# Output projection of a hybrid decoder block: half of its k tiles by seven block products

## The chip, the cores and the metric

The kernel runs on one core of one Trainium2 chip. The core has five engines that work side by side, each in the order of its own queue: TensorE (PE, matmuls), VectorE (DVE), ScalarE (ACT), GpSimd (POOL) and SyncE (SP, which here issues DMAs). The metric is the time of one execution in microseconds; lower is better.

## The reference, cut to what matters

One decoder layer for 512 tokens of width 1024. Two token mixers (a gated MLP and a sparse attention) are each projected to width 1024, merged by sigmoid gates, and sent through one output projection; a gated residual follows, then a second norm and the FFN. Everything is float32.

```
merged = sigmoid(g_a) * (y_a @ w_proj_a) + sigmoid(g_b) * (y_b @ w_proj_b)
x = x + gate1 * (merged @ w_out)                       # 512 x 1024 @ 1024 x 1024
h2 = rms_norm(x, norm2_g) * (1.0 + scale2) + shift2
f_g, f_u = split(h2 @ w_ffn_in)
x = x + gate2 * ((silu(f_g) * f_u) @ w_ffn_out)
```

## The kernel before

**Split products.** To keep float32 precision each operand is split into a high and a low part (`split`, L302: ScalarE copies the high part, VectorE subtracts it from the source for the low part), and `mm3` (L51) does three matmuls for one product: high x high, high x low, low x high. So every weight chunk needs two elementwise passes before TensorE can use it.

**The weight stream.** Weight chunks of 512 KB, and between them pieces of `w_ada` for the modulation vectors, stand in one list, `stream`, in the order of their use. `issue` (L72) puts a load on SP's queue into one of three `raw` buffers. `prep` (L95) makes the high and low part: into one of three rotating `hi`/`lo` pairs, or into a home of its own (`where`). `get(i)` (L142) hands out chunk i and, before that, makes sure (`ensure`, L117) that all entries up to two weight chunks ahead are prepared. So the order in which `prep`'s instructions lie on ScalarE's and VectorE's queues follows from where `get` is called. A buffer is known by its tag (`S2_2`, `E5`); a new tile on a tag waits until the last instruction that reads the old one, wherever that stands in the program.

**The order around the change.** The instructions of each engine run in the order in which the program lists them.

- Attention with `gb_part` (L1018) as filler ends with four sigmoids of the branch gates (L1064).
- *Projection B* (L1089): four groups of 256 output channels. In each, `opt_b` (L668) goes through two weight chunks (k tiles 0 to 3, then 4 to 7) with 24 matmuls each, the weights stationary and `yb` moving, all 512 tokens in one matmul. `yb` lies in the tiles with tags S2_0 to S2_7: high parts of k tiles 4 to 7 in S2_2 and S2_3, low parts in S2_6 and S2_7. After the second chunk `pb_evac` (L1075) multiplies by the gate, adds the other branch's part (`part`), and splits the merged tile into `mT`. `sec_tasks` (L362) does transposes of modulation pieces and a VectorE reduction into `Gc`; it has two such tasks in this stage. Low halves of the first chunk of each group are made on GpSimd (`pool=True`, L258), the others on VectorE.
- Then the pool `mid`, which holds the tiles of the first half of the program, is closed and the pool `ffn` opened on its memory (L1092).
- *Output projection* (L1239): merged tokens stationary, weights moving, 512 columns a matmul. Two halves of the tokens, in each of them two column halves `h` and four pairs of k tiles: 192 matmuls in 16 steps of 12. `resid` (L1101) multiplies by the gate, adds to the residual stream `xt` and squares for the norm. In the second half `row_rstd`, `norm2_x` and `norm2_T` (L1108 to L1130) normalise and transpose the first half's tokens; `norm2_T(0)` stands after the third of eight steps. `ensure(WF0[...])` and `s_prep` (L1194) prepare the first FFN weights there.
- *FFN input* (L1463) begins with the first half's tokens, and `norm2_T(1)` stands after 72 of its matmuls.

The FFN input and the first part of the FFN output run already by seven products instead of eight (`sprod` L1491, `zprod` L1592): with operands cut into 2 x 2 blocks, sums and differences of blocks are made beforehand, and results that several output blocks share are copied by ScalarE from one PSUM bank into another (`z_copy`) or kept in SBUF and added by VectorE (`z_add`).

## Time and profile before

| | |
|---|---|
| runs of the kernel before | 837.93, 837.97, 838.38 us (median 837.97) |
| the profiled execution | 838.1 us, of which the span of instructions is 836.2 |
| mean granted TensorE clock | 0.998 |
| HBM read and written | 105.90 MB, 2.10 MB |
| projection B | 396.1 to 441.2 us of the span |
| output projection | 441.2 to 487.4 us of the span |

A row of the timeline gives the start in us, the duration, the engine, the line of the kernel, the operation, output <- inputs, the shape and the count of instructions that were merged into the row; what stands in brackets is how long the engine had been idle before it and what ended that. A merged row's duration runs from the first start to the last end. A matmul's duration includes its way through the array, so two in a row overlap: their distance is read from the starts.

### The profile page before, as it was taken

The numbers are of one execution on the slowest core, as the hardware profiler recorded it, in microseconds if no ns is written. First come the engines' busy times: TensorE is split into PE (matmuls) and PEld (weight loads), VectorE is DVE, ScalarE is ACT, GpSimd is POOL, SyncE is SP. The second block draws the span as 40 slices with busy tenths as digits, with TensorE's granted clock in tenths as the row PEclk, the third lists the DMA queues.
The fourth block names the chain that finished last, engine by engine and source line by source line (L and its number), as shares of the span: only waits on it lengthen the run. The fifth ranks groups of instructions, "written<-read, shape, count | busy, mean of one in ns | idle before, by whom it ended". The sixth has DMA issues, their size and how long they took to land.

```text
span 836.2 us, 12860 instructions
## 1 busy us (share of the span) xinstructions
PE 824.3 (99%) x4992; PEld 733.8 (88%) x4992; DVE 666.7 (80%) x1147; ACT 401.8 (48%) x700; POOL 118.3 (14%) x105
## 2 busy tenths in 40 slices
PE   7999999999999999999999999999999999999996
PEld 7888989988888888988888899999999999888885
DVE  7968799788899638887786679889998888985635
ACT  6664435332232227665433556555555555663322
POOL 2060022353344411002210000000000000000001
PEclk9999999999999999999999999999999999999999
DMA  9962362423346551036544312445543335143212
GB/s 299 311 193 67 101 200 79 127 79 97 102 151 200 171 183 51 26 102 229 172 153 155 97 51 78 127 158 164 169 139 103 101 101 151 52 150 101 76 50 101
DMA packets 95676, 109.09 MB, mean 130 GB/s; under 512 B 5616, under 2 KB 76272, under 8 KB 95616
## 3 DMA queue, kind: packets, MB, share of 16 engines
q1 hardware_dynamic: 92512, 101.37, 38.8%
q0 software_dynamic: 2384, 6.10, 2.0%
q8 instruction: 39, 0.64, 0.3%
q10 hardware_dynamic: 720, 0.82, 0.3%
q14 instruction: 21, 0.17, 0.1%
HBM read 105.90 MB, written 2.10 MB: 129 GB/s over the span
## 4 chain that ended last, share of the span: by engine, by line
PE 95%; DMA 2%; SPq 1%; issue 0%; ACT 0%; DVE 0%; POOLq 0%; POOL 0%; ACTq 0%
PE pb L53 9%; PE pb L55 9%; PE pb L54 9%; PE R L53 8%; PE R L54 8%; PE R L55 8%; PE pfo L55 4%; PE pfo L53 4%; PE pfo L54 4%; PE pav L54 2%; PE pav L53 2%; PE pav L55 2%; PE pgb L53 2%; PE po L54 2%; PE pgb L54 2%; PE pgb L55 2%
## 5 line engine op out<-in xcount | busy, mean ns | idle before, releaser
L110 ACT ACTIVATE hi<-raw 128x1024 fp32r<-128x1024 f32 (+2 forms) x83 | 85.6, 1035 | 106.5 <-PE pfo L55 35.3
L114 POOL TENSOR_TENSOR lo<-raw,hi 128x1024 fp32r<-128x1024 f32 x33 | 83.3, 2528 | 212.7 <-ACT hi L110 199.1
L114 DVE TENSOR_TENSOR lo<-raw,hi 128x1024 fp32r<-128x1024 f32 (+2 forms) x43 | 53.3, 1244 | 51.0 <-ACT hi L110 50.9
L53 PE MATMUL pb<-h,hi 128*128 128x512 f32 x192 | 76.4, 398 | 0.0
L55 PE MATMUL pb<-h,lo 128*128 128x512 f32 x192 | 75.8, 395 | 0.0
L54 PE MATMUL pb<-hl,hi 128*128 128x512 f32 x192 | 75.8, 395 | 0.0
L55 PE MATMUL pfo<-hi,gs 128*128 128x512 f32 (+1 forms) x126 | 46.4, 369 | 0.0
L54 PE MATMUL pfo<-lo,gs 128*128 128x512 f32 (+1 forms) x126 | 46.4, 368 | 0.0
L53 PE MATMUL pfo<-hi,gs 128*128 128x512 f32 (+1 forms) x126 | 46.4, 368 | 0.0
L53 PE MATMUL R<-tb,sx 128*128 128x256 f32 x160 | 45.2, 282 | 0.0
L54 PE MATMUL R<-tb,sx 128*128 128x256 f32 x160 | 45.1, 282 | 0.0
L55 PE MATMUL R<-tb,sx 128*128 128x256 f32 x160 | 45.0, 281 | 0.0
L55 PE MATMUL R<-tb,lo 128*128 128x256 f32 x160 | 44.8, 280 | 0.0
L53 PE MATMUL R<-tb,hi 128*128 128x256 f32 x160 | 44.8, 280 | 0.0
L54 PE MATMUL R<-tb,hi 128*128 128x256 f32 x160 | 44.6, 279 | 0.0
L55 PEld LDWEIGHTS pb<-h,lo 128*128 128x128 f32 x192 | 36.0, 187 | 8.8
L54 PEld LDWEIGHTS pb<-hl,hi 128*128 128x128 f32 x192 | 36.0, 188 | 8.3
L53 PEld LDWEIGHTS pb<-h,hi 128*128 128x128 f32 x192 | 36.0, 188 | 8.3
L175 DVE SCALAR_TENSOR_TENSOR acc<-mraw,cols,acc 128x512 f32<-128x512 f32 x38 | 32.4, 853 | 8.3 <-DMA mraw<-in_w_ada_dram 7.5
L54 PE MATMUL pav<-lo,h 128*128 128x256 f32 x128 | 35.8, 279 | 0.0
L53 PE MATMUL pav<-hi,h 128*128 128x256 f32 x128 | 35.7, 279 | 0.0
L55 PE MATMUL pav<-hi,hl 128*128 128x256 f32 x128 | 35.7, 279 | 0.0
(377 smaller groups left out, 2647.9 us busy)
## 6 DMA issues: line engine op xcount, KB each, us to landing
raw<-in_w_ffn_in_dram SPq DMA_DIRECT2D x44, 512.0 KB, 4.3
raw<-in_w_in_dram SPq DMA_DIRECT2D x40, 512.0 KB, 3.7
mraw<-in_w_ada_dram SPq DMA_DIRECT2D x22, 512.0 KB, 3.8
raw<-in_w_ffn_out_dram SPq DMA_DIRECT2D x17, 512.0 KB, 3.6
s<-in_w_ada_dram SPq DMA_DIRECT2D x30, 256.0 KB, 5.6
raw<-in_w_ada_dram SPq DMA_DIRECT2D x10, 512.0 KB, 4.6
raw<-in_w_proj_a_dram SPq DMA_DIRECT2D x8, 512.0 KB, 4.7
raw<-in_w_proj_b_dram SPq DMA_DIRECT2D x8, 512.0 KB, 3.3
```

The costliest lines, as they stand in the source:

```text
L53: T.matmul(o, wh, rh, start=start, stop=False, **kw)
L54: T.matmul(o, wh, rlo, start=False, stop=False, **kw)
L55: T.matmul(o, wlo, rh, start=False, stop=stop, **kw)
L110: A.activation(hi[:, :m], e["raw"][:, :m], AF.Copy)
L114: e["lo"].tensor_sub(lo[:, :m], e["raw"][:, :m], f(hi[:, :m]))
L175: V.scalar_tensor_tensor(o, w, cs[:, j:j + 1], o, op0=OP.mult, op1=OP.add)
```

## The change

*Weights.* The stream keeps only the output weights of k tiles 4 to 7, four chunks; two of them get homes on the tags S2_2, S2_3 and S2_6, S2_7. The weights of k tiles 0 to 3 are four blocks B11, B12, B21, B22 (two k tiles by 512 columns), loaded at the start of projection B by four DMAs of their own (`o_issue`) into tiles of `mid`. The low halves of all projection-B chunks are made on VectorE.

*Preparation.* Eight steps (`O_STEPS`), one behind each chunk of projection B, make the differences of the weight blocks and of the merged token blocks, and split those that are needed first: B11, T1, A11, S1, T2, S2, A12, B21. `pb_evac` writes the merged result into `part` itself, and splits only k tiles 4 to 7.

*Products.* Seven products of 12 matmuls each (`oprod`), with copies between PSUM banks (`seed`), two kept results (`keep`, `add_kept`), and the remaining splits between them. The pool `mid` is closed after the seventh.

*The other k tiles* come on top, first half of the tokens, then second, with four steps of 12 matmuls in each; `norm2_T(0)` stands after the third step of the second half.

```diff
--- before.py
+++ after.py
@@ -101,6 +101,8 @@
         if e["where"] is None:
             hi = base.tile([128, 1024], F32R, name="hi", tag="hi", bufs=3)
             lo = base.tile([128, 1024], F32R, name="lo", tag="lo", bufs=3)
+        elif isinstance(e["where"], tuple):
+            hi, lo = (base.tile([128, 1024], F32R, name="wx", tag=t, bufs=1) for t in e["where"])
         else:
             t = ffn[0].tile([128, 2, 1024], F32R, name="wx", tag=e["where"], bufs=1)
             hi, lo = t[:, 0], t[:, 1]
@@ -255,10 +257,10 @@
         W_PA.append(group(w_pa, 256 * g, mods=mm_ if g < 3 else None, pool=2))
     W_GB = [group(w_in, 5192 + 256 * g, pool=2 * (g == 1), mods=mm_ if g > 1 else None, mraw=False) for g in range(4)]
     stream[W_GB[1][0]]["lo"] = V
-    W_PB = [group(w_pb, 256 * g, pool=True, mods=mm_ if g < 3 else None, mraw=False) for g in range(4)]
-    W_O = []
-    for n_, (h, k0) in enumerate(((0, 0), (1, 0), (0, 2), (1, 2), (0, 4), (0, 6), (1, 4), (1, 6))):
-        W_O.append((h, add_w(w_o, [k0, k0 + 1], 512 * h, 512, V, (None, None, None, "E2", "E0", "E1", "E3", "E4")[n_])))
+    W_PB = [group(w_pb, 256 * g, mods=mm_ if g < 3 else None, mraw=False) for g in range(4)]
+    W_O = [add_w(w_o, [k0, k0 + 1], 512 * h, 512, V, where) for h, k0, where in
+           ((0, 4, ("S2_2", "S2_3")), (0, 6, ("S2_6", "S2_7")), (1, 4, None), (1, 6, None))]
     mg = mod_sec(5)
     wh = ["E5", "E6", "E0", "E1"]
     W_F = [group(w_ffn_in, c, where=wh) for c in (0, DFF)]
@@ -680,7 +682,6 @@
                     midway()
             if i == W_PB[3][-1]:
                 sec_tasks(True)
-                ensure(W_O[2][1])
             if i == ids[-1]:
                 evac(pb)
             if post:
@@ -1067,30 +1068,75 @@
         P.dma_start(xt[i], x[i * 128:(i + 1) * 128, :])
-    mT = []
-    for m in range(8):
-        mT.append((base.tile([128, S], F32R, name=f"mh{m}", tag=f"S1_{m}", bufs=1),
-                   base.tile([128, S], F32R, name=f"ml{m}", tag=f"S1_{8 + m}", bufs=1)))
+    mT, om, ow, oraw = {}, {}, {}, {}
+    OM = {"A11": 0, "S1": 1, "S2": 2, "A12": 3, "S3": 0, "S4": 1, "A22": 2}
+    OW = {"B11": ("k_hi", "k_lo"), "T1": ("v_hi", "v_lo"), "T2": ("G0", "G1"), "T4": ("k_hi", "k_lo")}
+    def o_issue():
+        for n, (name, kh, h) in enumerate((("B11", 0, 0), ("B12", 0, 1), ("B22", 1, 1), ("B21", 1, 0))):
+            t = oraw[name] = mid.tile([128, 2, S], F32, name="oraw", tag=f"A{n}", bufs=1)
+            SY.dma_start(t, w_o[kh * 256:kh * 256 + 256, h * 512:h * 512 + 512].rearrange("(j p) n -> p j n", p=128))
+    def o_w(key, src):
+        if key in OW:
+            ow[key] = tuple(mid.tile([128, 2, S], F32R, name="ow", tag=t, bufs=1) for t in OW[key])
+        else:
+            ow[key] = tuple(base.tile([128, 2, S], F32R, name=t, tag=t, bufs=3) for t in ("hi", "lo"))
+        split(*ow[key], oraw[src])
+    def o_sub(o, a, b):
+        V.tensor_sub(oraw[o], oraw[a], oraw[b])
+    def m_block(key):
+        k, th = {"A11": (0, 0), "S2": (0, 0), "S3": (0, 0), "A21": (0, 1), "S1": (0, 1), "S4": (0, 1),
+                 "A12": (2, 0), "A22": (2, 1)}[key]
+        return part[0][:, k:k + 2, th * 256:(th + 1) * 256]
+    def o_m(key):
+        om[key] = tuple(base.tile([128, 2, 256], F32R, name="om", tag=f"S1_{OM[key] + 8 * e}", bufs=1) for e in range(2))
+        split(*om[key], m_block(key))
+    def o_sum(key):
+        if key == "S1":
+            V.tensor_add(m_block("S1"), m_block("A21"), m_block("A22"))
+        else:
+            a, b = {"S2": ("S1", "A11"), "S4": ("A12", "S2"), "S3": ("A22", "S2")}[key]
+            V.tensor_sub(m_block(key), m_block(a), m_block(b))
     def pb_evac(g):
         def ev(pb):
-            ts = {}
             for m in range(2):
                 k = 2 * g + m
-                t = ts[m] = t512("mg")
+                t, o = t512("mg"), part[k // 4][:, k % 4]
                 V.tensor_mul(t, pb[m], gbt[g][:, m])
-                V.tensor_add(t, t, part[k // 4][:, k % 4])
-                A.activation(mT[k][0], t, AF.Copy)
-            for m in range(2):
-                k = 2 * g + m
-                V.tensor_sub(mT[k][1], ts[m], f(mT[k][0]))
+                V.tensor_add(o, o, t)
+                if k >= 4:
+                    mT[k] = tuple(base.tile([128, S], F32R, name="mt", tag=f"S1_{k + 8 * e}", bufs=1) for e in range(2))
+                    A.activation(mT[k][0], o, AF.Copy)
+            for k in range(2 * g, 2 * g + 2):
+                if k >= 4:
+                    V.tensor_sub(mT[k][1], part[1][:, k % 4], f(mT[k][0]))
         return ev
+    O_STEPS = [[lambda: o_w("B11", "B11")],
+               [lambda: o_sub("B11", "B12", "B11"), lambda: o_w("T1", "B11")],
+               [lambda: o_sub("B11", "B22", "B11"), lambda: o_sub("B12", "B22", "B12")],
+               [lambda: o_sum("S1"), lambda: o_m("A11"), lambda: o_sum("S2"), lambda: o_m("S1"),
+                lambda: o_w("T2", "B11")],
+               [lambda: o_m("S2"), lambda: o_m("A12"), lambda: o_sum("S4")],
+               [lambda: o_sum("S3")],
+               [lambda: o_w("B21", "B21")], []]
+    def o_step():
+        for fn in O_STEPS.pop(0):
+            fn()
+    mbank[0] = 5
+    o_issue()
     for g in range(4):
-        opt_b(W_PB[g], 8, yb, nbanks(), pb_evac(g))
+        opt_b(W_PB[g], 8, yb, ((2, 3), (0, 1), (6, 7), (0, 1))[g], pb_evac(g), None, o_step)
     sec_tasks(True)
-    mid_stack.close()
-    ffn.append(ctx.enter_context(tc.tile_pool(name="ffn", bufs=1)))
     ss2 = base.tile([128, 4, 5], F32, name="ss2")
@@ -1233,40 +1279,82 @@
             V.tensor_sub(d["D"][1], rb, f(d["D"][0]))
         return [(a0, d0), (a1, d1), (a2, d2), (a3, d3)]
-    wch = {}
+    def seed(Z, ZB, dst, src):
+        Z[dst] = [bank(ZB[dst][e], "po") for e in range(2)]
+        for e in range(2):
+            A.activation(Z[dst][e], Z[src][e], AF.Copy)
+    def keep(Z, src, tag):
+        Z["s", src] = [t512("ps") if tag is None else base.tile([128, 512], F32, name="ps", tag=tag, bufs=2)
+                       for _ in range(2)]
+        for e in range(2):
+            A.activation(Z["s", src][e], Z[src][e], AF.Copy)
+    def add_kept(Z, dst, src):
+        for e in range(2):
+            V.tensor_add(Z[dst][e], Z[dst][e], Z["s", src][e])
+    O, OB = {}, ((4, 5), (6, 7), (0, 1), (2, 3))
+    def oprod(k, ka, kw, start):
+        if start:
+            O[k] = [bank(OB[k][e], "po") for e in range(2)]
+        (ah, al), (wh, wl) = om[ka], ow[kw]
+        for e in range(2):
+            o = slice(e * 128, (e + 1) * 128)
+            for j in range(2):
+                mm3(O[k][e], (ah[:, j, o], al[:, j, o]), (wh[:, j], wl[:, j]), start and j == 0, j == 1,
+                    skip_group_check=True)
     WF0 = W_F[0] + W_F[1]
-    OORD = (W_O, [W_O[n_] for n_ in (0, 2, 4, 5, 1, 3, 6, 7)])
+    oprod(0, "A11", "B11", True)
+    o_w("T3", "B12")
+    seed(O, OB, 1, 0)
+    oprod(3, "S1", "T1", True)
+    o_m("S3")
+    keep(O, 3, None)
+    o_w("B22", "B22")
+    oprod(1, "S2", "T2", False)
+    o_m("S4")
+    o_sub("B11", "B21", "B11")
+    seed(O, OB, 2, 1)
+    oprod(0, "A12", "B21", False)
+    o_w("T4", "B11")
+    o_m("A22")
+    oprod(2, "S3", "T3", False)
+    keep(O, 2, "acc")
+    oprod(1, "S4", "B22", False)
+    ensure(W_O[1])
+    oprod(2, "A22", "T4", False)
+    add_kept(O, 1, 3)
+    mid_stack.close()
+    ffn.append(ctx.enter_context(tc.tile_pool(name="ffn", bufs=1)))
+    ensure(W_O[3])
+    add_kept(O, 3, 2)
     for half in range(2):
-        po = {}
-        for n_, (h, i) in enumerate(OORD[half]):
-            if half == 0:
-                wch[i] = get(i, min(4, 7 - n_))
-            hi, lo = wch[i]
-            kts = stream[i]["kts"]
-            if kts[0] == 0:
-                po[h] = [bank(4 - 4 * half + 2 * h + e, "po") for e in range(2)]
-            for e in range(2):
-                opt_a_mm(po[h][e], 2 * half + e, hi, lo, kts, mT, 8)
-            if kts[0] == 6:
+        for h in range(2):
+            po = O[2 * half + h]
+            for n_, i in enumerate(W_O[2 * h:2 * h + 2]):
+                hi, lo = chunk[i]
                 for e in range(2):
-                    resid(po[h][e], 512 * h, 512, h, 2 * half + e, gate_b[1])
-            if half == 1:
-                if n_ == 1:
-                    for e in range(2):
-                        row_rstd(e)
-                    norm2_x(0)
+                    opt_a_mm(po[e], 2 * half + e, hi, lo, stream[i]["kts"], mT, 8, False)
+                if (half, h, n_) == (0, 0, 0):
                     ensure(WF0[1])
-                if n_ == 2:
-                    stream[WF0[2]]["lo"] = "later"
-                    norm2_T(0, {1: [lambda: ensure(WF0[2])],
-                                2: [lambda: stream[WF0[2]]["do"](), lambda: s_issue(-2)]})
-                if n_ == 3:
-                    stream[WF0[3]]["lo"] = "later"
+                if (half, h, n_) == (0, 1, 0):
                     ensure(WF0[3])
+                    s_issue(-2)
+                if (half, h, n_) == (1, 1, 0):
+                    norm2_T(0)
                     pre = s_prep(-2)
                     for fn in pre[0]:
                         fn()
-                    stream[WF0[3]]["do"]()
+            for e in range(2):
+                resid(po[e], 512 * h, 512, h, 2 * half + e, gate_b[1])
+        if half == 0:
+            for e in range(2):
+                row_rstd(e)
+            norm2_x(0)
     pre[1][0]()
     for e in range(2, 4):
         row_rstd(e)
```

## The prediction

> **What bounds the kernel now.** I read the page first: the busy line and the chain that ended last.
>
> ```profile
> span 836.2 us, 12860 instructions
> PE 824.3 (99%) x4992; PEld 733.8 (88%) x4992; DVE 666.7 (80%) x1147; ACT 401.8 (48%) x700; POOL 118.3 (14%) x105
> PE 95%; DMA 2%; SPq 1%; issue 0%; ACT 0%; DVE 0%; POOLq 0%; POOL 0%; ACTq 0%
> ```
>
> TensorE is busy for 99% of the span and carries 95% of the chain, so a matmul taken away is worth its issue time, and any hole that the change makes in TensorE's stream is paid in full: nothing later waits long enough to give it back. Then I cut the stretch that the change touches into projection B, output projection and start of the FFN, for all engines, and once more (last row) for the output projection's banks (`po`) alone.
>
> ```profile
> 396.10:441.20 45.10, 45.10 (x202) 36.85 (x201) 32.43 (x40) 17.68 (x21) 7.57 (x3) 1.00 0.52 171
> 441.20:487.40 46.20, 46.20 (x209) 37.73 (x208) 31.20 (x45) 21.70 (x34) 1.58 (x2) 1.00 0.33 103
> ...
> 441.20:487.40 46.20, 44.69 (x192) 35.79 (x191) 4.16 (x7) 1.00 0.33 103
> ```
>
> The columns after the length are busy us with counts of TensorE, its weight loads, VectorE, ScalarE and GpSimd; in the `po` row GpSimd and ScalarE have nothing and are left out. TensorE has no gap in either stage. VectorE is filled to 32.4 of 45.1 us in projection B, so it has room on average; whether it has it at the right moment is the question. One 512-column matmul issues every 44.69 / 192 = 0.233 us.
>
> **What it removes from TensorE.** Four k tiles cost 8 block products of 12 matmuls (2 token tiles, 2 k tiles, 3 split terms), now 7: 12 x 0.233 = 2.79 us less. The rest of the count is unchanged: 84 + 96 matmuls against 192.
>
> **VectorE in projection B.** Rows for its pieces, and, in the second fence, GpSimd's low half that runs beside the pair at 410.71:
>
> ```profile
> 404.00 2.58 DVE L114 TENSOR_TENSOR lo<-raw,hi 128x1024 fp32r<-128x1024 f32 x1 [2.37 <-ACT hi L110]
> ...
> 410.71 3.55 DVE L175 SCALAR_TENSOR_TENSOR acc<-raw,cols,acc 128x512 f32<-128x512 f32 x2
> 414.18 0.68 DVE L389 TENSOR_REDUCE Gc<-mod 128x4 f32<-128x512 f32 x1
> ...
> 415.17 1.53 DVE L175 SCALAR_TENSOR_TENSOR acc<-raw,cols,acc 128x512 f32<-128x512 f32 x2
> ...
> 442.33 1.23 DVE L114 TENSOR_TENSOR lo<-raw,hi 128x1024 fp32r<-128x1024 f32 x1 [4.17 <-ACT hi L110]
> 443.47 0.68 DVE L1081 TENSOR_TENSOR mg<-pb,gb 128x512 f32<-128x512 f32 x1
> 444.19 0.69 DVE L1082 TENSOR_TENSOR mg<-mg,part 128x512 f32<-128x512 f32 x1
> 444.80 0.68 DVE L1081 TENSOR_TENSOR mg<-pb,gb 128x512 f32<-128x512 f32 x1
> 445.51 0.69 DVE L1082 TENSOR_TENSOR mg<-mg,part 128x512 f32<-128x512 f32 x1
> 446.12 1.47 DVE L1086 TENSOR_TENSOR ml<-mg,mh 128x512 fp32r<-128x512 f32 x2
> ...
> 447.86 3.50 DVE L114 TENSOR_TENSOR wx<-raw,wx 128x1024 fp32r<-128x1024 f32 x3
> ```
> ```profile
> 411.15 2.56 POOL L114 TENSOR_TENSOR lo<-raw,hi 128x1024 fp32r<-128x1024 f32 x1 [5.66 <-ACT hi L110]
> ```
>
> Read as prices from start to start: a 1024-wide subtraction 1.14 us ((3.50 - 1.23) / 2, from three in a row and one alone), a pair of accumulations 1.45, the `Gc` reduction with its two small operations 1.0 (414.18 to 415.17), a column group's multiply-add-multiply-add 2.65 (443.47 to 446.12), a 512-wide operation about 0.65 (0.61 to 0.78 in the last rows but one). The pair at 410.71 took 3.55 us while GpSimd ran its low half, and 1.53 us alone: the low halves on GpSimd were not free for VectorE. So moving one onto VectorE costs 1.14 us and gives about 2 back; this edit by itself saves. The Trainium skill, "SBUF — State Buffer", section "Who interferes with whom", says a VectorE instruction with two SBUF inputs and a GpSimd one that reads SBUF exclude each other for a whole instruction; the rows agree with that.
>
> The seven-product part adds far more to VectorE here than it takes. ScalarE is in its four sigmoids until the first projection-B high halves:
>
> ```profile
> 398.17 3.91 ACT L1064 ACTIVATE gb<-gb 128x1024 f32<-128x1024 f32 x4
> 401.97 2.00 ACT L110 ACTIVATE hi<-raw 128x1024 fp32r<-128x1024 f32 x2
> ```
>
> so VectorE, in order behind the first low half, starts at about 403.0. Up to the end of the low half of group 3's first chunk its queue then holds: five low halves of projection B, those of B11, T1 and T2, and three weight differences, 11 x 1.14 = 12.5; four pairs of accumulations, 5.8; two groups' evacuation, 5.3; `Gc`, 1.0; S1, S2 and the lows of A11 and S1, 4 x 0.65 = 2.6; and 1.1 in which T1's low half waits for its high half on ScalarE, which waits for the difference. Sum 28.3, end at 431.3. TensorE wants that low half in the third matmul of group 3:
>
> ```profile
> 396.14 0.39 PE L53 MATMUL pb<-yb,hi 128*128 128x512 f32 x1
> ...
> 429.69 0.40 PE L53 MATMUL pb<-yb,hi 128*128 128x512 f32 x1
> ```
>
> that is at 429.69 + 2 x 0.233 = 430.2. **First hole: 1.2 us** (0 if the queue is 4% shorter; 3 if the loads of output weights land late or the differences wait). Groups 1 and 2 get their low halves about 2 us ahead by the same list, so nothing is lost there. The loads I cost at nothing: the same output weights move, half of them earlier. Four issues stand on SP's queue at the end of attention, at about 396, ahead of group 1's second weight chunk, which TensorE reads at 396.14 + 72 x 0.233 = 412.9; B11 is first used at 403. Work of VectorE covers both; a late one adds its lateness to this hole.
>
> **The wait that is added.** `get` looks two chunks ahead, so at group 3's first chunk ScalarE is handed the high half of W_O[0] and VectorE its low half. Their new homes, S2_2 and S2_3, hold `yb` of k tiles 4 to 7, which TensorE reads until the end of group 3 (T, 441.2 plus the first hole). A new tenant waits for the last reader, and the queue stands still behind it; the trace has the same for a weight slot, with ScalarE idle for 4.87 us:
>
> ```profile
> 441.23 1.06 ACT L110 ACTIVATE hi<-raw 128x1024 fp32r<-128x1024 f32 x1 [4.87 <-PE pb L54]
> ...
> 444.91 0.63 ACT L1083 ACTIVATE mh<-mg 128x512 fp32r<-128x512 f32 x1 [2.62 <-DVE mg L1082]
> ```
> ```profile
> 716.67 0.58 ACT L1607 ACTIVATE pfo<-pfo 128x512 f32<-128x512 f32 x1 [2.26 <-PE pfo L55]
> ```
>
> Queued behind it on VectorE: B21's low half, the second `Gc`, W_O[1]'s low half, group 3's evacuation; on ScalarE behind that: two copies of merged tiles, T3's high half, and then the copies that seed product bank 1 from bank 0 (the last row above is such a copy in the FFN). From T: 0.2 until the last matmul is done, 3 x 1.14 + 1.0 = 4.4, multiply-add-multiply-add to the end of the second add 2.7, ScalarE's copy 0.65, T3's high half 1.0, the first seed 0.6: T + 9.55. TensorE has only two products that need none of this, A11 x B11 and S1 x T1, 24 x 0.233 = 5.6 us; S2 x T2 adds onto the seed. **Second hole: 3.95 us.** Bank 5, which the second `Gc` still reads, also holds back half of the first product, but inside this hole. From below 3.0, if `Gc` runs before the wait (0 is a rival's case); from above 5, with 0.3 us of hand-over at four of the steps. I take the sum of the rows. Afterwards each product's operands come before TensorE asks (seed of bank 2 at T + 13.9, wanted at T + 15.2; T4 at T + 17.5, wanted at T + 20.8).
>
> **The tail.** The second half of the tokens now has four weight chunks, not eight, and `norm2_T(0)` stands after the third: 12 matmuls, 2.8 us, follow it, where 5 x 2.8 followed before. Behind it on VectorE stand its own evacuation, three operations of `s_prep`, and the last residual, which `norm2_T(1)` needs.
>
> ```profile
> 487.47 0.28 PE L53 MATMUL pf<-h,wx 128*128 128x256 f32 x1
> ...
> 496.04 1.91 PE L1147 MATMUL x2T<-cst,xn 128*128 128x128 f32 x16
> 497.71 0.36 PE L53 MATMUL pf<-h,wx 128*128 128x256 f32 x1
> ```
> ```profile
> 487.36 0.68 DVE L1104 TENSOR_TENSOR rt<-po,gate1b 128x512 f32<-128x512 f32 x1
> ...
> 496.68 1.00 DVE L1157 TENSOR_SCALAR h2f<-x2T,Gc 128x256 f32<-128x256 f32 x2 [1.11 <-PE x2T L1147]
> ...
> 502.09 0.69 DVE L1162 TENSOR_TENSOR h<-h2f,h 128x512 fp32r<-128x512 f32 x1 [0.43 <-ACT h L1159]
> ...
> 515.76 0.69 DVE L1209 TENSOR_TENSOR raw<-raw 128x512 f32<-128x512 f32 x1
> ...
> 517.70 1.22 DVE L1218 TENSOR_TENSOR sx<-raw,sx 128x1024 fp32r<-128x1024 f32 x1
> ```
> ```profile
> 492.21 1.15 ACT L1126 ACTIVATE xn<-xr,sm 128x1024 f32<-128x1024 f32 x1 [0.34 <-POOL sm L1110]
> ```
>
> From the start X of the first transposes VectorE needs 6.65 for the evacuation (496.04 to 502.7), 1.95 for `s_prep` (515.76 to 517.70), and from the first residual multiply to the scaled rows 6.0 (487.36 to 493.36): X + 14.6. TensorE is there at 1.67 (transposes, 496.04 to 497.71) + 2.8 + 8.57 (487.47 to 496.04) = X + 13.0. **Third hole: 1.6 us** (0 to 3, as VectorE comes to X without or with a backlog; by the same kind of list it is free 0.4 us after X).
>
> **Sum.** -2.79 + 1.2 + 3.95 + 1.6 = +3.96 us. The profiled execution took 838.1 us (span 836.2 and 1.9 around it), 0.13 above the median of 837.97, so the forecast is 841.9.
>
> **Rivals.** *The seeds come in time (faster).* If the three lows and `Gc` did not stand before group 3's evacuation, the seed would come at T + 5.15, ahead of the 5.6 us of cover, and the second hole is gone; the point is 4.4 us of VectorE work in front. With VectorE also 1.2 us ahead in projection B and 1.6 us ahead at X, all 2.79 us stay: 835.2. For it: VectorE is free for 12.7 of 45.1 us in the first stage. Against: the free time lies where it stands waiting for T.
> *Only the middle hole.* Lists of 28.3 and 14.6 us are long; 4% and 11% off them close the first and third hole, and -2.79 + 3.95 = +1.16 gives 839.1, which is no difference within 0.2%.
> *The clock falls.* The trace shows it after the last matmul:
>
> ```profile
> 829.00:831.00 2.00, 0.30 (x3) 0.09 (x1) 1.39 (x5) 0.80 (x3) 0.00 (x0) 1.00 0.69 262
> 831.00:832.00 1.00, 0.00 (x0) 0.00 (x0) 0.56 (x2) 0.27 (x1) 0.66 (x1) 1.00 0.00 0
> 832.00:833.00 1.00, 0.00 (x0) 0.00 (x0) 0.28 (x1) 0.34 (x1) 0.00 (x0) 0.61 0.00 0
> 833.00:834.00 1.00, 0.00 (x0) 0.00 (x0) 0.00 (x0) 0.00 (x0) 0.00 (x0) 0.50 0.86 331
> ```
>
> The third column from the end is the granted clock: full until about 3 us after TensorE stops, then half. If the second hole were whole, as long as that, and the return took as long, TensorE would lose half of 3.3 us: 841.9 + 1.65 = 843.5. Against it, bank 5 parts the hole into 1.9 and 2.1 us, and below 3 us the rows show full clock. The Trainium skill, "TensorE: Matmul & The Clock Gate", Part 1, gives an idle window of about 3.4 us for the fall and as much work for the return, an estimated 1.7 us here; the rows agree for the fall, and none shows the return.
>
> **How the numbers follow.** Forecast 0.6; seeds in time 0.15; only the middle hole 0.13; clock 0.12. The three holes' bounds with the 2.79 us give +0.2 (0, 3.0, 0) to +8.2 (3, 5, 3). The range, 837.8 to 845.2, holds the low end, the middle hole's 839.1 and the clock's 843.5, and leaves out the faster case and the corner in which everything is late at once. A measurement of this kernel can tell 0.2%, 1.7 us. Faster 0.15, same 0.14 (the middle hole and the low corner of the forecast), slower 0.71.
>
> **What would show it.** Right: TensorE idle before `pb<-yb` at group 3, released by `lo` on VectorE; idle before `po<-om,ow` in the second product, released by ScalarE's copy into `po`; a wait of `x2T` for `xn`; VectorE idle until group 3 ends, then three lows before `mg<-pb`; the pair of accumulations at 1.5 us throughout; a clock of 1.00. Wrong: no TensorE idle above 0.5 us in the products, or W_O[0]'s low half run before group 3 ends.

## The result and the profile after

| | before | after |
|---|---|---|
| runs | 6, median 838.04 us (837.86 to 838.55) | 6, median 844.68 us (844.22 to 847.27) |
| profiled execution, span | 838.1, 836.2 | 844.57, 842.8 |
| projection B | 45.1 | 47.9 |
| output projection | 46.3 | 47.3 |
| start of the FFN | 24.5 | 26.1 |

The change makes the kernel slower: ratio 1.0085, 95% interval 1.0072 to 1.0099. The forecast was 841.9, with a range of 837.8 to 845.2. From the page after, the busy line and the chain that ended last:

```profile
PE 822.8 (98%) x4980; PEld 731.1 (87%) x4980; DVE 679.4 (81%) x1169; ACT 410.0 (49%) x714; POOL 107.9 (13%) x101
PE 85%; DVE 8%; ACT 2%; DMA 2%; issue 1%; SPq 0%; POOL 0%; POOLq 0%; DVEq 0%; ACTq 0%
```

There are 12 matmuls fewer, but VectorE, which was at 0% of the chain, now has 8% of it. That share counts all of VectorE's work along which the chain runs; it is not the time lost, which the views below give. The view of the stages (length, then busy time and count of TensorE, weight loads, VectorE, ScalarE and GpSimd, then the granted clock), cut at the first matmul of projection B, of the output projection, of the FFN, and of the FFN's seven-product loop (`R`):

```profile
396.09:444.02 47.93, 45.58 (x203) 36.65 (x201) 36.10 (x48) 20.76 (x25) 0.00 (x0) 1.00 0.54 174
444.02:491.27 47.25, 43.68 (x198) 35.35 (x196) 36.35 (x52) 24.63 (x42) 1.58 (x2) 1.00 0.29 89
491.27:517.34 26.07, 25.04 (x209) 24.64 (x208) 22.56 (x35) 17.54 (x29) 2.07 (x3) 1.00 0.25 82
517.34:547.34 30.00, 29.30 (x246) 28.89 (x245) 27.23 (x38) 17.40 (x32) 0.00 (x0) 1.00 0.22 71
```

The same cuts in the profile before:

```profile
396.13:441.21 45.08, 45.08 (x202) 36.82 (x201) 32.43 (x40) 17.65 (x21) 7.57 (x3) 1.00 0.52 171
441.21:487.47 46.26, 46.26 (x209) 37.76 (x208) 31.27 (x45) 21.70 (x34) 1.58 (x2) 1.00 0.32 103
487.47:512.00 24.53, 24.53 (x209) 24.52 (x208) 20.50 (x31) 16.85 (x28) 2.07 (x3) 1.00 0.32 108
512.00:542.00 30.00, 30.00 (x256) 30.00 (x255) 27.06 (x37) 16.34 (x29) 0.00 (x0) 1.00 0.25 80
```

TensorE is busy all the time there. So projection B is 2.85 us longer after the change, the output projection 0.99 (that is -2.79 for the matmuls and +3.78 of hole), the start of the FFN 1.54. The spans differ by 6.6, which leaves 1.2 for the loop: from its first matmul to the last of the program it takes 317.0 us before and 318.2 after. The holes have names in the view of TensorE's waits (us in total, times, longest). It counts idle time alone, so its numbers are somewhat smaller than the differences of the stages.

```profile
PE pb L55 <- DVE lo L116: 2.4, 1, 2.4
PE po L53 <- DVE Gc L391: 1.8, 1, 1.8
PE po L53 <- ACT po L1286: 1.8, 1, 1.8
PE x2T L1193 <- ACT xn L1172: 1.0, 1, 1.0
...
PE R L53 <- ACT R L1618: 0.5, 1, 0.5
PE R L53 <- ACT ps L1636: 0.2, 1, 0.2
```

The first four rows are the three holes of the forecast, the second one in the two parts that were foretold; the last two are a fourth that was not. The rows of the timeline behind them, first hole first (SP's queue, ScalarE, VectorE):

```profile
394.37 3.54 SPq L1079 DMA_DIRECT2D oraw<-in_w_out_dram  x4
398.74 0.37 SPq L92 DMA_DIRECT2D raw<-in_w_proj_b_dram  x1
...
406.87 1.06 ACT L112 ACTIVATE hi<-raw 128x1024 fp32r<-128x1024 f32 x1 [2.95 <-DMA raw<-in_w_proj_b_dram]
...
407.97 1.23 DVE L116 TENSOR_TENSOR lo<-raw,hi 128x1024 fp32r<-128x1024 f32 x1 [1.41 <-ACT hi L112]
...
430.14 1.53 DVE L177 SCALAR_TENSOR_TENSOR acc<-raw,cols,acc 128x512 f32<-128x512 f32 x2
431.58 1.22 DVE L116 TENSOR_TENSOR lo<-raw,hi 128x1024 fp32r<-128x1024 f32 x1
```

The weight chunk issued at 398.74 (the second of group 1), behind four loads of 512 KB, lets ScalarE go on at 406.87, 8.1 us later. VectorE stands still for 1.41 us, and the low half that TensorE wants at 430.2 begins only at 431.58. The second hole (VectorE, ScalarE, TensorE):

```profile
444.27 1.23 DVE L116 TENSOR_TENSOR wx<-raw,wx 128x1024 fp32r<-128x1024 f32 x1 [3.88 <-ACT hi L305]
...
446.55 0.68 DVE L391 TENSOR_REDUCE Gc<-mod 128x4 f32<-128x512 f32 x1
...
447.55 1.23 DVE L116 TENSOR_TENSOR wx<-raw,wx 128x1024 fp32r<-128x1024 f32 x1
...
450.14 0.63 ACT L1116 ACTIVATE mt<-part 128x512 fp32r<-128x512 f32 x1 [5.68 <-DVE part L1113]
...
452.95 1.06 ACT L1286 ACTIVATE po<-po 128x512 f32<-128x512 f32 x2
...
453.58 0.50 PE L53 MATMUL po<-ow,om 128*128 128x512 f32 x1 [1.76 <-ACT po L1286]
```

VectorE waits until projection B has ended (its first row names ScalarE's high half, but that was done at 443.50, and the last matmul of projection B starts only just before 444.02), makes three low halves and `Gc`, and only then merges; ScalarE idles for 5.68 us before the merged tiles and copies the seed at 452.95. The third and the fourth:

```profile
499.84 1.23 DVE L1264 TENSOR_TENSOR lo<-raw,hi 128x1024 fp32r<-128x1024 f32 x1
501.10 1.23 DVE L1265 TENSOR_TENSOR raw<-raw 128x1024 f32<-128x1024 f32 x1
502.27 1.22 DVE L1272 TENSOR_TENSOR lo<-raw,hi 128x1024 fp32r<-128x1024 f32 x1
503.42 0.99 DVE L1203 TENSOR_SCALAR h2f<-x2T,Gc 128x256 f32<-128x256 f32 x2
...
522.49 0.69 DVE L1255 TENSOR_TENSOR raw<-raw 128x512 f32<-128x512 f32 x1
...
501.35 0.33 PE L1193 MATMUL x2T<-cst,xn 128*128 128x128 f32 x1 [1.03 <-ACT xn L1172]
...
531.22 0.39 PE L53 MATMUL R<-tb,sx 128*128 128x256 f32 x1 [0.48 <-ACT R L1618]
```

VectorE is not only late for the rows of `xn`: three preparations of FFN weights stand before it can scale the transposes at 503.42, and it reaches the loop's first difference (`raw<-raw`) at 522.49, 5.15 us after the loop's start at 517.34. Before the change it was there 3.76 us after it (515.76 against 512.00). The experiments show that the fourth hole follows this lateness.

### The profile page after: what moved, and what is told of

Its sections match the earlier page's. It is cut to its first block, busy times and chain, and to the rows that moved or that the text cites. A ratio compares the mean times of both kernels' runs of the same rounds, so it can differ in the third digit from the quotient of the medians.

```text
span 842.8 us, 12864 instructions
## 1 busy us (share of the span) xinstructions
PE 822.8 (98%) x4980; PEld 731.1 (87%) x4980; DVE 679.4 (81%) x1169; ACT 410.0 (49%) x714; POOL 107.9 (13%) x101
## 4 chain that ended last, share of the span: by engine, by line
PE 85%; DVE 8%; ACT 2%; DMA 2%; issue 1%; SPq 0%; POOL 0%; POOLq 0%; DVEq 0%; ACTq 0%
PE R L53 7%; PE pb L55 7%; PE R L54 7%; PE pb L53 7%; PE R L55 7%; PE pb L54 7%; PE pfo L55 4%; PE pfo L54 4%; PE pfo L53 4%; PE pav L54 2%; PE pav L53 2%; PE pav L55 2%; PE pgb L53 2%; PE pgb L54 2%; PE pgb L55 2%
## 5 line engine op out<-in xcount | busy, mean ns | idle before, releaser
L112 ACT ACTIVATE hi<-raw 128x1024 fp32r<-128x1024 f32 (+2 forms) x82 | 84.5, 1034 | 101.1 <-PE pfo L55 35.2
L116 DVE TENSOR_TENSOR lo<-raw,hi 128x1024 fp32r<-128x1024 f32 (+2 forms) x46 | 55.5, 1212 | 48.5 <-ACT hi L112 48.3
L116 POOL TENSOR_TENSOR lo<-raw,hi 128x1024 fp32r<-128x1024 f32 x29 | 72.9, 2517 | 127.6 <-ACT hi L112 122.0
L54 PE MATMUL R<-tb,sx 128*128 128x256 f32 x160 | 45.1, 282 | 0.0
```

The costliest lines, as they stand in the source:

```text
L54: T.matmul(o, wh, rlo, start=False, stop=False, **kw)
L112: A.activation(hi[:, :m], e["raw"][:, :m], AF.Copy)
L116: e["lo"].tensor_sub(lo[:, :m], e["raw"][:, :m], f(hi[:, :m]))
```

## The experiments

Each kernel was timed beside the kernel before, on the same chip.

**The low halves on VectorE alone.**

```diff
-    W_PB = [group(w_pb, 256 * g, pool=True, mods=..., mraw=False) for g in range(4)]
+    W_PB = [group(w_pb, 256 * g, mods=..., mraw=False) for g in range(4)]
```

> The kernel before with one part of the change alone: all low halves of projection B's weights are computed on VectorE, none on GpSimd. Theory (the holes come from the seven-product work queued on VectorE, not from the low halves): no TensorE hole in projection B, the pair of accumulations falls from 3.55 to about 1.5 us, and the time stays where it was, 838.0 +-0.5. Rival (the low halves on VectorE are themselves a cost): a TensorE hole of 1 us or more ahead of some group of projection B, 839 or more.

838.99 us, ratio 1.0010 (1.0001 to 1.0018). No TensorE hole: projection B takes 45.08 us as before, and VectorE's busy time in it falls from 32.43 to 30.61 us. The pair of accumulations takes 1.53 us each time.

```profile
395.97:441.05 45.08, 45.08 (x203) 36.81 (x201) 30.61 (x43) 17.76 (x21) 0.00 (x0) 1.00 0.49 161
```

So the theory holds for the stage, and the edit spares VectorE 1.8 us. The total is 0.9 above before, a little outside the theory's 0.5 and at the edge of the rival's 839, but the rival's hole is not there: in the trace the excess lies behind the last matmul (8.1 us from its start to the end of the span against 7.2), and why stays open.

**The low halves back on GpSimd.**

```diff
-    W_PB = [group(w_pb, 256 * g, mods=..., mraw=False) for g in range(4)]
+    W_PB = [group(w_pb, 256 * g, pool=True, mods=..., mraw=False) for g in range(4)]
```

> The changed kernel with that one part undone: the low halves of projection B's first weight chunks are on GpSimd again, the seven-product part stays. Theory (seven-product work on VectorE and its loads make the first hole): the first hole stays at 2 to 3.5 us, the pair of accumulations slows to 3 us or more wherever GpSimd runs a low half beside it, and the time is that of the changed kernel, 844.7, or up to 1.5 more. Rival (the low halves on VectorE make the first hole): the hole of 2.4 us before group 3 is gone and the time is about 842.

846.86 us, ratio 1.0100 (1.0085 to 1.0114). The rival falls: TensorE's waits in projection B grow from 2.4 to 3.3 us (0.60 in group 2; 0.66 and 1.98 in group 3). Rows of GpSimd, VectorE and TensorE at group 3:

```profile
431.38 2.63 POOL L116 TENSOR_TENSOR lo<-raw,hi 128x1024 fp32r<-128x1024 f32 x1 [13.20 <-ACT hi L112]
...
431.72 3.63 DVE L177 SCALAR_TENSOR_TENSOR acc<-raw,cols,acc 128x512 f32<-128x512 f32 x2
...
434.07 0.50 PE L55 MATMUL pb<-yb,lo 128*128 128x512 f32 x1 [1.98 <-POOL lo L116]
```

The pair takes 3.63 us beside GpSimd, against 1.53 in the changed kernel. So the low halves on VectorE do not make the first hole; beside the seven products they shorten it. The time says less: it is 0.7 above the theory's range, and its interval overlaps with that of the changed kernel (1.0072 to 1.0099). The profiled execution also lost 1.7 us at half clock from about 435.5 on (last section). By itself the move brought no gain in time, as the run before showed.

**Two loads later.**

```diff
-    O_STEPS = [[lambda: o_w("B11", "B11")],
+    O_STEPS = [[lambda: o_w("B11", "B11"), lambda: o_issue((2, 3))],
...
-    o_issue()
+    o_issue((0, 1))
```

> The changed kernel, with two of the four early loads of output weights (B22 and B21) issued one step later, so that the load of projection B's second weight chunk is not queued behind all four. Theory (the first hole, 2.86 us instead of the 1.2 forecast, has 1.4 us from that late load): the load lands in about 4 us instead of 8, VectorE's idle of 1.41 us near 408 us goes, the first hole falls to about 1.4 us and the time to about 843.2. Rival (VectorE's own list is longer than forecast and the load only fell into slack): first hole still 2.5 us or more, time 844.7.

843.21 us, ratio 1.0063 (1.0051 to 1.0075), 1.5 us below the changed kernel. ScalarE's row for the late chunk, and the stage:

```profile
404.33 1.06 ACT L112 ACTIVATE hi<-raw 128x1024 fp32r<-128x1024 f32 x1 [0.65 <-DMA raw<-in_w_proj_b_dram]
```
```profile
395.85:442.21 46.36, 45.28 (x202) 36.74 (x201) 36.00 (x48) 20.87 (x25) 0.00 (x0) 1.00 0.56 180
```

The chunk is there 5.8 us after its issue at 398.50, later than the 4 us of the theory but early enough: VectorE makes its low half without a gap, and the stage's excess over 45.08 falls from 2.85 to 1.28, next to the 1.2 that the forecast had. The load explains what the forecast missed of the first hole. This profiled execution is the slowest of the five (844.33); the clock fell in it for a while, which cost 1.7 us (last section).

**W_O[0] and W_O[1] later.**

```diff
-            hi, lo = get(i)
+            hi, lo = get(i, min(2, wseq.index(W_PB[3][1]) - wseq.index(i)) if i in W_PB[3] else 2)
```

> The changed kernel, with the preparation of the output projection's first two plain weight chunks moved out of projection B's last group to after the sixth product, so that nothing on VectorE and ScalarE waits there for the end of projection B. Theory (VectorE's low halves and Gc in front of the evacuation make the second hole): both waits of 1.8 us in the products go, output projection 3.77 us shorter, time about 840.9; if ScalarE's and VectorE's work is late behind the sixth product instead, up to 1 us of it comes back there. Rival (the products are bound by the seeds and by ScalarE's own work in any order): a wait of 2 us or more stays in the products, 843 to 844.7.

The profiled execution took 842.51 us and has neither wait in the products. Its output projection takes 44.57 us, 2.68 less than in the changed kernel; about 1.1 of the 3.78 come back in its tail, where `x2T` now waits for `xn` of the first token half too, and another 0.5 in the start of the FFN (26.58 against 26.07); the theory had allowed up to 1. The six runs spread from 842.13 to 845.80, median 844.63 (1.0071, 1.0058 to 1.0084). The two shortest, 842.13 and 842.51, have a mean granted clock of 0.998, the other four 0.993 to 0.997: the other holes are still there, and the clock seems to have fallen behind them. So the waits decide for the theory, but the median misses its 840.9 and lies in the rival's range; by the time alone this run settles nothing.

**Both, with the seven-product steps in another order.**

```diff
-               [lambda: o_sum("S1"), ..., lambda: o_w("T2", "B11")],
-               [lambda: o_m("S2"), lambda: o_m("A12"), lambda: o_sum("S4")],
-               [lambda: o_sum("S3")],
-               [lambda: o_w("B21", "B21")], []]
+               [],
+               [lambda: o_sum("S1"), lambda: o_m("A11"), lambda: o_sum("S2"), lambda: o_m("S1")],
+               [lambda: o_m("S2"), lambda: o_m("A12"), lambda: o_sum("S4"), lambda: o_sum("S3")],
+               [lambda: o_w("T2", "B11")], []]
```

The two edits before are in it too, and B21's split and the seeds are reordered between the products.

> The changed kernel with both front holes attacked by order alone: the two late loads and the later preparation of the two plain weight chunks as in the runs before, and the seven-product work of projection B's steps shifted so that none of it stands ahead of group 3's first low half that the products do not need at once (token sums and the splits of A11 and S1 behind it, T2 last; B21's split and the seeds between the products). Theory (order of VectorE's queue): first and second hole gone, so 844.7 - 2.9 - 3.8 = 838.0, with the tail's and the FFN's 2.7 still there; with no hole of 2 us left the clock stays full and the runs lie within 1 us of each other. Rival (VectorE simply has too much work up to the end of the products): 2 us or more of waits show up again at group 3 or in the products, 840 or more.

840.41 us (840.17 to 840.58), ratio 1.0025 (1.0016 to 1.0035).

```profile
396.40:441.48 45.08, 45.08 (x203) 36.82 (x201) 37.41 (x52) 18.48 (x22) 0.00 (x0) 1.00 0.55 185
441.48:486.76 45.28, 43.61 (x197) 35.45 (x196) 34.60 (x48) 26.68 (x43) 1.57 (x2) 1.00 0.29 93
486.76:513.34 26.58, 25.11 (x209) 24.63 (x208) 23.07 (x36) 18.01 (x30) 2.06 (x3) 1.00 0.25 80
```

Projection B is as short as before the change, with VectorE busy for 37.41 of 45.08 us instead of 32.43, and the products have no wait. Both front holes are gone, by order alone, and the spread of the runs shrinks from 3 us to 0.4. The time is 2.4 above the theory's 838.0 and so within the rival's "840 or more", but the rival's waits at group 3 and in the products are not there: the tail holes grew. The output projection is 1.8 us above 46.26 - 2.79 and the FFN's start 2.05 above before: TensorE comes to the tail earlier, VectorE does not to the same extent, and now both normalisations wait.

```profile
PE x2T L1195 <- ACT xn L1174: 2.3, 2, 1.2
```

**The tail alone, and with the front.** The seventh product moves behind the first token half, and two FFN preparation steps and `norm2_T(0)` ahead of the second half's residuals.

```diff
+    o_resid(0, 1)
...
+    norm2_x(0)
+    oprod(2, "A22", "T4", False)
+    pre = s_prep(-2)
...
+    o_top(1, 0, 0)
+    o_top(1, 0, 1)
+    norm2_T(0)
+    o_resid(1, 0)
```

> The changed kernel with only its tail reordered: the seventh product is moved behind the first token half's plain chunks, its weights in slots of the outer pool, and the FFN's first two preparation steps stand ahead of the second half, so that VectorE has about 8 us more before the second normalisation is needed. Theory (third and fourth hole are VectorE's backlog from the tail, carried into the FFN): the x2T wait of 1.0 us and the gaps of 0.5 and 0.8 us at the start of the FFN loop go, 844.7 - 1.5 - 1.2 = 842.0. Rival (the fourth hole is the FFN preparation's own and independent of the third): x2T wait gone but the FFN gaps stay, 843.2.

> Both edits together, front and tail. Theory (four holes, all from the order of the queues): all of them gone, and the 12 matmuls of 0.233 us that the seven products save show: 838.1 - 2.8 = 835.3. Rival (the seven products cost VectorE and ScalarE more than the stage has, whatever the order): a hole of 1 us or more remains and the time is 836.5 or above.

851.32 us, 1.0155 (1.0141 to 1.0169), and 844.87 us, 1.0082 (1.0068 to 1.0095): both misses. In the first of them TensorE and VectorE show why:

```profile
497.78 0.55 PE L53 MATMUL pf<-h,wx 128*128 128x256 f32 x1 [3.62 <-DVE rt L1150]
...
496.95 0.68 DVE L1150 TENSOR_TENSOR rt<-po,gate1b 128x512 f32<-128x512 f32 x1
```

The FFN's first matmuls write the banks that the second half's residuals read, and those stood behind the whole scaling of the first half on VectorE. My order took away one wait and put a larger one in its place. The wait is not the whole loss: in the profiled execution of the first kernel the granted clock stood at half three times, behind the waits of 2.3 us (group 3), 1.8 us (`Gc`) and 3.62 us, and by windows of 0.5 us this cost 1.7, 1.7 and 3.2 us, together more than the wait; the changed kernel's profile has no such stretch. So the 851.32 us do not measure the order alone. The second kernel lost 1.7 us in the same way. One thing came out of it: in both kernels the loop is as short as before the change (317.0 us from its first matmul to the last of the program), and VectorE reaches the loop's first difference 3.76 and 3.77 us after the loop's start.

**The tail, worked out from the trace.**

```diff
     o_sub("B11", "B21", "B11")
+    ensure(W_O[0])
     oprod(0, "A12", "B21", False)
     o_w("T4", "B11")
...
+    ensure(W_O[3])
+    add_kept(O, 3, 2)
+    ensure(WF0[0])
+    o_resid(0, 0)
...
+    ensure(WF0[2])
+    o_resid(0, 1)
...
+    norm2_x(0)
+    oprod(2, "A22", "T4", False)
+    ensure(WF0[3])
+    pre = s_prep(-2)
...
+    o_top(1, 0, 0)
+    o_top(1, 0, 1)
+    o_resid(1, 0)
+    norm2_T(0)
```

> The kernel with the front reordered, and a tail worked out again from its trace. W_O[0] is prepared in VectorE's free 1.1 us ahead of T4, so the loads behind it start earlier; the two FFN low halves that stood ahead of the first token half's last residual move behind it; the seventh product stands between the token halves; the first FFN preparation step comes before the second half's residuals. Theory (the tail holes are VectorE work waiting in the wrong place): norm2_T(0) and norm2_T(1) wait less than 0.5 us each, the FFN loop has no gap, and the time is 838.1 - 2.8 = 835.3, up to 836.3 if the second normalisation is up to 1 us late. Rival (VectorE has 4 to 5 us more work between products and FFN than TensorE leaves, in any order): 2 us or more of holes stay between the last product and the FFN loop, 837.5 or more.

840.23 us, 1.0021 (1.0012 to 1.0030): no better, and within the rival's 837.5 or more. In the profiled execution (840.62) 1.7 us of it were lost at half clock behind the hole at 487 us (last section). VectorE in this kernel has two large gaps in the stretch in which it is late:

```profile
470.20 2.36 DVE L116 TENSOR_TENSOR wx<-raw,wx 128x1024 fp32r<-128x1024 f32 x2 [1.74 <-ACT wx L112]
...
479.47 1.22 DVE L116 TENSOR_TENSOR wx<-raw,wx 128x1024 fp32r<-128x1024 f32 x1 [2.58 <-ACT wx L112]
```

Both times ScalarE made the high half behind something that itself waited (the squares of a residual, the rows scaled by a GpSimd result). That gave the next edit. `sqs` holds the residual's squares back on ScalarE, and with "later" `ensure` makes the high half alone and `do` the low half:

```diff
     seed(O, OB, 1, 0)
+    o_sub("B11", "B21", "B11")
     o_w("B21", "B21")
...
-    o_sub("B11", "B21", "B11")
     ensure(W_O[0])
...
-    o_resid(0, 0)
+    o_resid(0, 0, sqs)
+    ensure(WF0[2])
+    for fn in sqs:
+        fn()
...
+    stream[WF0[3]]["lo"] = "later"
+    ensure(WF0[3])
     for e in range(2):
         row_rstd(e)
     norm2_x(0)
+    stream[WF0[3]]["do"]()
```

> The last version with three more moves that only fill VectorE's idle stretches of that trace: the difference for T4 goes to the start of the products (1.09 us idle there), the high halves of two FFN chunks go ahead of the squares of the first residual on ScalarE (1.74 us of VectorE idle), and the fourth FFN high half goes ahead of the row scales (2.58 us idle, of which about 1.2 come back). Theory (VectorE is late in the tail by its idle stretches, not by its amount of work): VectorE reaches the scaling of the first normalisation about 4 us earlier (485.2 before), the holes of 0.63, 1.74 and 0.73 us between the last product and the FFN go, the FFN loop's 0.6 us goes or halves, 835.3 to 836.3. Rival (amount of work): VectorE arrives at most 2 us earlier and 1.5 us or more of holes stay, 837.5 or more.

834.86 us (834.82 to 835.26), ratio 0.9961 (0.9946 to 0.9975): the version that beats both kernels. After the start of the program TensorE waits for 0.6 us in all, in the modulation, and the stages are

```profile
396.28:441.36 45.08, 45.08 (x203) 36.83 (x201) 37.41 (x52) 18.47 (x22) 0.00 (x0) 1.00 0.55 184
441.36:484.54 43.18, 43.18 (x197) 35.50 (x196) 37.55 (x53) 28.61 (x47) 1.58 (x2) 1.00 0.31 98
484.54:509.07 24.53, 24.53 (x210) 24.53 (x208) 21.23 (x33) 17.40 (x29) 2.06 (x3) 1.00 0.27 87
509.07:539.07 30.00, 30.00 (x256) 30.00 (x255) 27.10 (x37) 16.37 (x29) 0.00 (x0) 1.00 0.25 79
```

The output projection is 3.08 us shorter than before the change, the 2.79 of the 12 matmuls and 0.3 more that were not traced; the other stages are as before. Of the 5.5 us between the profiled executions of this version and the last, 1.7 are the clock, which does not fall here. The rival (too much work for VectorE in any order) is refuted: VectorE's busy time in the whole span is 679.3 us here and 679.4 in the changed kernel, and it reaches the scaling of the first normalisation at 479.52 instead of 485.20.

**One low half moved behind the second normalisation.**

```diff
     pre[1][1]()
-    for fn in pre[2]:
-        fn()
...
                     norm2_T(1)
-                    for fn in pre[3]:
+                    for fn in pre[2] + pre[3]:
                         fn()
```

> The same with one 1024-wide low half (the FFN's third preparation step) moved behind the second normalisation. Theory: the second normalisation's scaling starts 1.2 us earlier on VectorE, but the same work is in front of the FFN loop, so the time is within 0.3 us of the version without this move. Rival (the first FFN chunks after the second normalisation are what waits): up to 0.6 us faster.

836.01 us, 0.9974 (0.9964 to 0.9983): 1.15 us slower than without it, and the theory's 0.3 is missed. On VectorE the row that had followed back to back now has a gap:

```profile
493.62 0.99 DVE L1210 TENSOR_SCALAR h2f<-x2T,Gc 128x256 f32<-128x256 f32 x2 [0.98 <-PE x2T L1200]
```

The transposes were not there yet. One idle microsecond on VectorE, 15 us ahead of the loop, comes back as one microsecond of TensorE in it (318.0 us against 317.0), in gaps that end at 517.55 and 522.56. VectorE's first difference is 4.90 us behind the loop's start (513.84 against 508.94), 3.80 without the move.

Taken together, these kernels show what makes the fourth hole. Where VectorE reaches the loop's first difference 3.76 to 3.80 us after the loop's start, the loop takes 317.0 us to the last matmul; at 4.55 us (the version at 840.23) 317.6, at 4.90 318.0, at 5.15 (the changed kernel) 318.2. The hole follows VectorE's lateness, not the loop itself.

## Why the prediction was right, and where it was off

The forecast was 841.9, the measured median is 844.68, inside the range. Direction, places and releasers of the three holes were right; the sum was 2.8 us short. That the range still held is in part luck: its upper end had room for a late load, but the fourth hole was in none of its bounds.

*The gain of 2.79 us* is there, as the last kernels show: output projection 46.26 to 43.18.

*First hole, 1.2 forecast, 2.85 measured.* The mechanism and the place were right (`pb` at group 3, released by VectorE's `lo`). The mis-sized term is the load: the prediction cost the four early issues at nothing and said that a late one adds its lateness here. It did: VectorE's idle 1.41 us, and 1.28 us of hole once two loads go later. The list itself was right: in that run group 3's low half ends 35.2 us after the start of projection B, where the forecast had 431.3 against 396.1, the same 35.2.

*Second hole, 3.95 forecast, 3.78 measured*, in two parts of 1.81 (`Gc`, bank 5) and 1.76 us (seed), where 1.9 and 2.1 were forecast. The order behind the wait on VectorE and ScalarE was that of the prediction, and the first matmul on the seeded bank started 9.56 us after the end of projection B (453.58 against 444.02), where T + 9.55 was forecast for the seed. One detail was off without consequence: the high half of W_O[0] did not have to wait for the end of projection B, ScalarE made it at 441.50, 2.5 us earlier; its low half did wait.

*Third hole, 1.6 forecast, 1.54 measured*, with the wait of `x2T` for `xn` as said. The agreement is better than the working: the wait itself is 1.03 us, 1.2 by the starts of the matmuls. From the first transposes (486.78) to the scaled rows (501.29) the list took 14.5 us, where 14.6 was forecast, but TensorE was there after 13.4 us, not 13.0; the other 0.3 us of the stage lie outside this wait.

*The step that failed* is the end of the argument: after the second normalisation the prediction counted nothing, although by its own third hole VectorE is late there. VectorE carried its backlog through the FFN's start, and 1.2 us came out in the loop, where VectorE is busy for 27.1 of the first 30 us even without a backlog (last row of the stages of the 834.86 us version). The sum with the sizes measured is -2.79 + 2.85 + 3.78 + 1.54 + 1.2 = +6.6, the difference of the spans.

*The low halves on VectorE* spare VectorE time, as forecast: 1.53 us a pair throughout, and 3.63 with GpSimd back. The rule of the Trainium skill that the prediction weighed ("SBUF — State Buffer", "Who interferes with whom") agrees with that run.

*The rivals.* "The seeds come in time" is what the reordered kernels make true, and its 835.2 is close to the 834.86 measured in the best of them; in the changed kernel it failed for the reason given, VectorE's free time lies where it stands waiting. "Only the middle hole" did not happen. "The clock falls" was set aside because bank 5 parts the hole. The profiled execution of the changed kernel has a clock of 1.00 in all four stages, so the fall is no part of the 6.6 us there; but that reason was too strong, as the last section shows. The price that the prediction put on a fall, 1.65 us, was about right: most falls in these traces cost 1.7 us.

## What to carry to other kernels

When a change saves time on one engine by giving work to others, list the other engines' queues instruction by instruction up to the point of use, and follow the backlog to the next place where the queue is empty, not only to the next wait: a microsecond of idle on a 90%-busy VectorE came out as a microsecond of TensorE 24 to 29 us later. Before giving work away or dropping the idea, look for idle stretches in that queue: the same instructions in another order turned +6.6 us into -3.4. Loads issued early for later use are free only if nothing that is needed sooner is queued behind them.

## What the runs showed of the hardware

*The clock can fall after holes well below 3 us.* The prediction had read from the profile before that it falls about 3 us after TensorE stops. In the version at 840.23 us a gap of 1.73 us between two starts (1.34 of it idle), with one of 0.73 right behind it, sufficed, and the fall came about 2 us after the first matmul behind the gap (487.25):

```profile
486.00:487.00 1.00, 0.00 (x0) 0.00 (x0) 0.19 (x1) 0.97 (x3) 0.00 (x0) 1.00 0.00 0
...
489.00:490.00 1.00, 1.00 (x8) 1.00 (x7) 0.82 (x3) 0.98 (x2) 0.00 (x0) 0.61 0.00 0
490.00:491.00 1.00, 1.00 (x6) 1.00 (x6) 0.58 (x2) 0.73 (x2) 0.00 (x0) 0.50 0.00 0
...
492.00:493.00 1.00, 1.00 (x8) 1.00 (x8) 0.96 (x3) 0.14 (x1) 0.00 (x0) 0.68 0.00 0
```

In the kernel with two loads later the two waits of 1.81 and 1.76 us, with 4.2 us of matmuls between them, brought the clock down in the profiled execution:

```profile
450.00:455.00 5.00, 3.24 (x9) 2.59 (x9) 3.22 (x7) 5.00 (x9) 0.00 (x0) 0.71 0.00 0
```

Eight matmuls that start from 452.12 to 455.11 lie 0.43 us apart there instead of 0.233. In both of these traces, and in that of the kernel with the low halves back on GpSimd (behind its wait of 1.98 us), the clock stood at half for 3.4 us, with TensorE busy, and that cost 1.7 us; behind the wait of 3.62 us in the version at 851.32 us it was 6.8 us, at a cost of 3.2. The changed kernel has the same two waits at a clock of 1.00 in its profile, so the same waits do not always bring it down; what decides was not tested. This would fit the spread of the changed kernel's runs (844.2 to 847.3) and the narrow one of the kernels without holes. The Trainium skill, "TensorE: Matmul & The Clock Gate", Part 1, says that activity is counted in a free-running window of about 3.4 us, which would agree with that; that one idle window of that length is needed for the fall does not agree with the 1.73 us here.

*A load waits for what stands before it on the queue*: a load of 512 KB was there 8.1 us after its issue behind four such loads of output weights, and 5.8 us behind two.
